# Weighted one-hots for four tokens at a time in a scatter by matmul

## The chip, the cores and the metric
The kernel runs on one core of one Trainium2 chip, as one program. The metric is the device time of one execution in microseconds. TensorE (PE) does the matmuls, VectorE (DVE) and ScalarE (ACT) the elementwise work, GpSimd (POOL) some gathers, SyncE (SP) starts most transfers. Each engine works through its own queue in order, and semaphores hold an instruction until what it reads has been written and what it overwrites has been read.

## The reference
One decoder layer on a sequence of 1024 tokens of width 1024: a gMLP and an S5 state space branch with an output projection, then a retrieval layer with 8 heads over 16384 experts (128 x 128 product keys), then a final norm. The retrieval layer is what matters here:

```
s = einsum('thcd,hckd->thck', q, keys); top_s, top_i = top_k(s, 16)
cand_s = top_s[:, :, 0, :, None] + top_s[:, :, 1, None, :]      # 16 x 16 sums of a head
best_s, pos = top_k(cand_s, 16); idx = the experts of these;  g = softmax(best_s)
act = gelu(einsum('thkd,td->thk', u_tab[idx], t));  y = einsum('thk,thkd->td', g * act, v_tab[idx])
```

Each token so has 128 (8 x 16) pairs of an expert index and a weight g. All arithmetic is in float32.

## The kernel before
Tokens are worked on in 8 blocks of 128. The last three go the way of the reference: the rows of their experts are gathered by GpSimd, multiplied and summed (`side_work`). For the first five (640 tokens) the kernel computes all 16384 experts densely on TensorE, and needs their weights as a matrix G of tokens by experts that is zero where an expert wasn't chosen.

The first third of the span is the two branches, then come output projections (`outproj`), scores (`score`) and routes (`route`, with `topk`: runs of MAX8, FIND_INDEX8 and MATCH_REPLACE8 on VectorE). A route gives for each token 128 first key numbers (`I32t`), 128 second ones (`J16`) and 128 weights (`gT`), transposed so that a column is a token and its 128 choices lie across the partitions. `scatter` (L678 and on) makes G from them. It takes eight tokens at a time:

- `hot` (L685): one VectorE operation compares the number of a column with `J16`; fp16, [128, 128 keys, 8 tokens], the tokens innermost. So one token's one-hot lies in every eighth element, 16 bytes apart.
- `a1` (L690): VectorE, for four tokens at a time, the one-hot of the first key; fp32, token by token in a row. Two buffers.
- `b1` (L694 or L698): the one-hot of the second key times the weight. For a pair of tokens either VectorE makes it in one operation of 256 elements, or ScalarE in two activations of 128. Which one is set by a number for each block, `dv`: every dv-th pair is VectorE's. Six buffers of two tokens.
- L700: for each token one product of `b1` and `a1` on TensorE, 128 x 128, which the trace shows as two matmul instructions; L703: ScalarE copies the results of eight tokens to `GS` in two operations; L706: SyncE stores 32 tokens' worth in `G_d`.

After the scatter come the pairs of dense stages: `stage1` (L959, products with the first table and gelu), `weigh` (L978, times G) and `stage2` (L997, L1006, products with the second table), over 128 groups of experts, with `side_work` between them. `stage1` of the first five groups may run ahead of the last scatter.

The order in which pieces of the blocks' work are issued (routes r0 to r7, scatters s0 to s4, scores, projections) comes from the table `plan` in CFG: a start and a length for each item, into which its steps are spread. A scheduler that simulates the engines then orders the instructions of each queue. The routes of gather blocks 5 and 6 are issued among the last scatters; they read their scores back from memory (`scr`) in buffers that share the tag `hs` with `hot`.

Of the kernel before, what the change touches and what calls it, by code (L numbers as in the profile page):

```python
# [8 lines left out]
F32 = mybir.dt.float32  # L9
# [6 lines left out]
AF = mybir.ActivationFunctionType  # L16
ALU = mybir.AluOpType
# [4 lines left out]
P = 128  # L22
# [16 lines left out]
QG = 4  # L39
GP = 2  # L40
FMAX = 3.0e38
CFG = dict(xo=[2, 3, 4, 0, 1], gt=3, ss=7, hs=2, b1=6, nw=6, raw=1, ngb=3, rows=4, lead=5, per=6.3, dv=[6, 9, 9, 2, 99], early=2,
           hp=600, eo=(2, 4), em={2: 'pppxx', 4: 'Xpp'}, seg=4, plan=dict(
    op0=(-238.2, 44.5), sb0=(-21, 248.8), m5=(-490.1, 3.4), r0=(234.1, 82.1), op1=(132.1, 27.3), op2=(292.7, 7.7),
    sb1=(310, 10.8), op3=(364.9, 36.8), r1=(301.9, 79), s0=(261.5, 137.5), sb2=(303.2, 61.7), zv=(372.6, 16.7),
# [3 lines left out]
    gt=(858.2, 122), rel=(739, 334), s4=(981.8, 131.5), r5=(916.4, 58.6), r6=(989.9, 124.6), ld=(776, 675.7),  # L49
# [11 lines left out]
def bcast(ap, axis, n):  # L61
    shape = list(ap.shape)
    shape.insert(axis, n)
    idx = [slice(None)] * len(ap.shape)
    idx.insert(axis, None)
    return ap[tuple(idx)].to_broadcast(shape)
# [30 lines left out]
@with_exitstack  # L97
def tile_hybrid_layer(ctx: ExitStack, tc: tile.TileContext, a, out, cfg=CFG):
    nc = tc.nc
    V, A, G, T = nc.vector, nc.scalar, nc.gpsimd, nc.tensor  # L100
# [25 lines left out]
    def bankB(name):  # L126
        return psB.tile([P, 2, 512], F32, tag="b", name=name)
# [43 lines left out]
    def slotS(shape, name, dt=F32):  # L171
        return sS.tile(shape, dt, tag="k8", name=name)
# [36 lines left out]
    early = {}  # L209
# [351 lines left out]
    ss = []  # L561
# [116 lines left out]
    def scatter(b, I32t, J16, gT):  # L678
        t0 = b * P
        for q in range(4):  # L680
            GS = [slotS([P, NE // 2, 32], f"GS{b}_{q}_{i}") for i in range(2)]
            for t8 in range(4):
                s1 = q * 32 + t8 * 8
                hot = kp.tile([P, P, 8], F16, tag="hs", name=f"hot{b}_{s1}", bufs=cfg["hs"])
                V.tensor_tensor(hot, iot8, bcast(J16[:, s1:s1 + 8], 1, P), op=ALU.is_equal)  # L685
                pg = bankB(f"pgs{b}_{s1}")
                for o in range(8):
                    if o % 4 == 0:
                        a1 = kp.tile([P, 4, P], F32, tag="a1", name=f"a1_{b}_{s1 + o}", bufs=2)
                        V.tensor_tensor(a1, bcast(iot, 1, 4), bcast(I32t[:, s1 + o:s1 + o + 4], 2, P), op=ALU.is_equal)  # L690
                    if o % 2 == 0:
                        b1 = kp.tile([P, 2, P], F32, tag="b1", name=f"b1_{b}_{s1 + o}", bufs=cfg["b1"])
                        if (s1 + o) // 2 % cfg["dv"][b] == 0:
                            V.tensor_tensor(b1, hot[:, :, o:o + 2].rearrange("p j t -> p t j"),  # L694
                                            bcast(gT[:, s1 + o:s1 + o + 2], 2, P), op=ALU.mult)
                        else:
                            for n in range(2):
                                A.activation(b1[:, n], hot[:, :, o + n], AF.Copy,  # L698
                                             scale=gT[:, s1 + o + n:s1 + o + n + 1])
                    T.matmul(pg[:, o // 4, (o % 4) * P:(o % 4 + 1) * P], b1[:, o % 2], a1[:, o % 4], start=True, stop=True)  # L700
                pgv = pg.rearrange("p a (t i) -> p i (a t)", t=4)
                for i in range(2):
                    A.copy(GS[i][:, :, t8 * 8:t8 * 8 + 8], pgv[:, i * 64:(i + 1) * 64])  # L703
                yield
            for i in range(2):
                nc.sync.dma_start(G_d[i * 16:(i + 1) * 16, :, b * 4 + q, :].rearrange("g p c -> p g c"),  # L706
                                  GS[i].rearrange("p (g e) t -> p g (e t)", e=QG))
# [93 lines left out]
    def put(b):  # L801
        yield from scatter(b, *ijg.pop(b))
# [243 lines left out]
    def lead(i0, i1):  # L1046
        for i in range(i0, i1):
            yield from stage1(i)
# [23 lines left out]
    def prep_steps(n):  # L1072
# [17 lines left out]
        gt=(gt2_row, 1, "m5"), rel=(release, NDB, "gt op7 sb7"), ld=(lambda: lead(0, L), 2 * L, "rel"))  # L1090
# [13 lines left out]
    while left:  # L1104
# [3 lines left out]
        _, n, need = items[item]  # L1108
# [384 lines left out]
```

## Time and profile before

| | us |
|---|---|
| median of 3 runs | 2657.55 (2655.81 to 2659.86) |
| the profiled execution | 2655.86 |
| its span, first to last instruction | 2653.9 |
| TensorE busy | 2538.1 (96%) |
| VectorE busy | 2267.8 (85%) |
| ScalarE busy | 1312.8 (49%) |
| GpSimd busy | 1180.9 (44%) |

Shares of busy time are means over stages that differ: the stretches are in the first group of the rows below. Scatter instructions run from 354 to 860 us. A duration in a row is that of one instruction; on a full engine the next one starts before the last has quite ended, so the distance from start to start is shorter. A wait names who was late, by the profile's inference from semaphores.

### The profile page before, as it was taken

Reading aid. Unit: us, or ns where it says so; the run is one execution under the profiler, and the core shown is the slowest. Engines: PE = TensorE matmul, PEld = TensorE weight load, DVE = VectorE, ACT = ScalarE, POOL = GpSimd, SP = SyncE. Lnnn points to the kernel's source line nnn. Section 1 sums busy time; section 2 is a strip of 40 time slices with the busy share of each in tenths; the row PEclk is TensorE's granted clock in tenths of the full one; section 3 lists DMA queues with packets and bytes.
Section 4 is the critical chain, followed back from the end, with each engine's and each line's share of the span. In section 5 each row is a group of like instructions: output and inputs, shape, how many; then the busy total and the mean of one; then the engine's idle time right before and its main releaser. Section 6 shows DMA issues by size and latency. Waiting matters only on the chain. (4 is left out here: it accounts for less than half of the span.)

```text
span 2653.9 us, 39049 instructions
## 1 busy us (share of the span) xinstructions
PE 2538.1 (96%) x14119; PEld 2168.1 (82%) x14119; DVE 2267.8 (85%) x4215; ACT 1312.8 (49%) x2315; POOL 1180.9 (44%) x842
## 2 busy tenths in 40 slices
PE   6999999999877999999999999999999999999997
PEld 2548677678666898989999989999999988999986
DVE  7984699869899888789989888889999888899898
ACT  2311246568868377773222577762223767732222
POOL 0001000000000177676667578766665767776660
PEclk9996999999988999999999999999999999999999
DMA  9546233444636699999999999899998999999993
GB/s 362 108 121 217 101 122 104 126 136 135 181 118 193 218 328 326 343 327 364 341 340 375 325 336 330 331 354 364 341 355 326 334 345 343 325 368 345 343 365 139
DMA packets 301761, 726.85 MB, mean 274 GB/s; under 512 B 42448, under 2 KB 133072, under 8 KB 301152
## 3 DMA queue, kind: packets, MB, share of 16 engines
q0 software_dynamic: 112832, 411.09, 42.4%
q1 hardware_dynamic: 165600, 254.48, 28.6%
q10 hardware_dynamic: 23136, 58.79, 6.2%
q8 instruction: 111, 1.82, 0.3%
q14 instruction: 82, 0.67, 0.1%
HBM read 660.70 MB, written 62.39 MB: 272 GB/s over the span
## 5 line engine op out<-in xcount | busy, mean ns | idle before, releaser
L888 POOL DMA_INDIRECT ru<-in_peer_u_dram,ix x384 | 637.7, 1661 | 897.6 <-issue 745.1
L959 PE MATMUL pa<-Th,u 128*128 128x320 f32 x4096 | 911.3, 310 | 4.9 <-DVE u L936 3.1
L959 PEld LDWEIGHTS pa<-Th,u 128*128 128x128 f32 x4096 | 688.4, 188 | 8.7 <-DVE u L936 3.6
L888 POOL DMA_INDIRECT rv<-in_peer_v_dram,ix x384 | 522.8, 1361 | 257.4 <-DVE gacc L916 168.0
L959 PE MATMUL pa<-Tl,u 128*128 128x320 f32 x2048 | 633.4, 309 | 0.0
L899 DVE TENSOR_TENSOR ru<-ru,hn 128x2048 f32<-128x2048 f32 x192 | 438.6, 2289 | 113.1 <-DMA ru<-in_peer_u_dram,ix 106.6
L894 ACT ACTIVATE jk<-ru 128x1024 bf16<-128x1024 f32 x384 | 405.4, 1056 | 213.2 <-issue 167.7
L916 DVE SCALAR_TENSOR_TENSOR gacc<-rv,act,gacc 128x1024 f32<-128x1024 f32 x381 | 489.2, 1284 | 6.4 <-DVE u L936 0.4
L1006 PE MATMUL pd<-v,wh 128*128 128x512 f32 x1280 | 402.6, 390 | 3.2 <-ACT wh L980 1.6
L997 PE MATMUL res<-v,wh 128*128 128x512 f32 x1280 | 400.7, 390 | 0.8 <-ACT wh L980 0.8
L959 PEld LDWEIGHTS pa<-Tl,u 128*128 128x128 f32 x2048 | 385.3, 188 | 1.7
L1006 PEld LDWEIGHTS pd<-v,wh 128*128 128x128 f32 x1280 | 238.8, 188 | 52.5 <-ACT wh L980 2.5
L997 PEld LDWEIGHTS res<-v,wh 128*128 128x128 f32 x1280 | 239.6, 188 | 50.4 <-ACT wh L980 1.6
L961 ACT ACTIVATE w<-pa 128x320 f32<-128x320 f32 x256 | 108.7, 431 | 333.7 <-PE pa L959 311.9
L698 ACT ACTIVATE b<-hot,gT 128x128 f32<-128x128 f16 x520 | 233.5, 537 | 61.0 <-PE pgs L700 36.0
L1006 PE MATMUL pd<-v,wl 128*128 128x512 f32 x640 | 248.7, 390 | 1.7 <-DVE wl L982 1.6
L997 PE MATMUL res<-v,wl 128*128 128x512 f32 x640 | 248.1, 389 | 1.3 <-DVE wl L982 1.3
L935 ACT CAST u<-ur 128x1024 fp32r<-128x1024 f32 x128 | 133.5, 1043 | 205.3 <-DMA ur<-in_peer_ut_dram 79.0
L700 PE MATMUL pgs<-a,b 128*128 128x128 f32 x1280 | 188.9, 299 | 46.2 <-DVE a L690 19.3
L700 PEld LDWEIGHTS pgs<-a,b 128*128 128x128 f32 x1280 | 169.9, 207 | 68.4 <-ACT b L698 35.3
L936 DVE TENSOR_TENSOR u<-ur,u 128x1024 fp32r<-128x1024 f32 x128 | 156.3, 1221 | 29.7 <-ACT u L935 23.2
L943 ACT CAST v<-vr 128x1024 fp32r<-128x1024 f32 x128 | 133.7, 1045 | 94.1 <-DMA vr<-in_peer_v_dram 76.8
(349 smaller groups left out, 3050.4 us busy)
## 6 DMA issues: line engine op xcount, KB each, us to landing
vr<-in_peer_v_dram SPq DMA_DIRECT2D x128, 512.0 KB
ur<-in_peer_ut_dram SPq DMA_DIRECT2D x128, 512.0 KB
G_d<-GS SPq DMA_DIRECT2D x40, 1024.0 KB
Gt<-G_d ACTq DMA_DIRECT2D x64, 640.0 KB
wada<-in_w_ada_dram SPq DMA_DIRECT2D x17, 1024.0 KB
wo<-in_w_out_dram SPq DMA_DIRECT2D x8, 1024.0 KB
ru<-in_peer_u_dram,ix POOLq DMA_INDIRECT x384
rv<-in_peer_v_dram,ix POOLq DMA_INDIRECT x384
```

The source lines that it names most:

```text
L698: A.activation(b1[:, n], hot[:, :, o + n], AF.Copy, scale=gT[:, s1 + o + n:s1 + o + n + 1])
L700: T.matmul(pg[:, o // 4, (o % 4) * P:(o % 4 + 1) * P], b1[:, o % 2], a1[:, o % 4], start=True, stop=True)
L888: G.indirect_dma_start(out=row[:, e], out_offset=None, in_=a[src], in_offset=bass.IndirectOffsetOnAxis(ap=ix[:, s0 + e:s0 + e + 1], axis=0))
L894: A.activation(junk, row[:, e], AF.Copy, accum_out=act[:, s + e:s + e + 1])
L899: V.tensor_mul(row, row, bcast(hn, 1, GP))
L916: V.scalar_tensor_tensor(ac, row[:, e], w, ac, op0=ALU.mult, op1=ALU.add)
L935: A.copy(u[:, 0], ur)
L936: V.tensor_tensor(u[:, 1], ur, u[:, 0].bitcast(F32), op=ALU.subtract)
L943: A.copy(v[:, 0], vr)
L959: T.matmul(pa[:, :NN], l[:, k, :], r[:, k, ns], start=(k == 0 and m == 0), stop=(k == KD - 1 and m == 2))
L997: T.matmul(res[tb][n], l[:, ts], r[:, n * 512:(n + 1) * 512], start=(g == 0 and q == 0 and m == 0), stop=(g == NGR - 1 and q == QG - 1 and ...
L1006: T.matmul(po, l[:, ts], r[:, n * 512:(n + 1) * 512], start=(q == 0 and m == 0), stop=(q == QG - 1 and m == 2))
```

## The change
`b1` of two tokens becomes `b4` of four, with three buffers in place of six. Where VectorE makes it, one operation of 512 elements covers four tokens: the loop over keys is the outer one and that over tokens the inner one, so it reads four fp16 values in a row of `hot` and the four weights, and writes each value to another token's row, 512 bytes on. ScalarE's activations are as before, one for each token. The numbers `dv` now count quads, and are 3, 4, 4, 1, 3 where they were 6, 9, 9, 2, 99 for pairs. The plan is the same.

```diff
-CFG = dict(xo=[2, 3, 4, 0, 1], gt=3, ss=7, hs=2, b1=6, nw=6, raw=1, ngb=3, rows=4, lead=5, per=6.3, dv=[6, 9, 9, 2, 99], early=2,
+CFG = dict(xo=[2, 3, 4, 0, 1], gt=3, ss=7, hs=2, b4=3, nw=6, raw=1, ngb=3, rows=4, lead=5, per=6.3, dv=[3, 4, 4, 1, 3], early=2,
...
-                    if o % 2 == 0:
-                        b1 = kp.tile([P, 2, P], F32, tag="b1", name=f"b1_{b}_{s1 + o}", bufs=cfg["b1"])
-                        if (s1 + o) // 2 % cfg["dv"][b] == 0:
-                            V.tensor_tensor(b1, hot[:, :, o:o + 2].rearrange("p j t -> p t j"),
-                                            bcast(gT[:, s1 + o:s1 + o + 2], 2, P), op=ALU.mult)
-                        else:
-                            for n in range(2):
-                                A.activation(b1[:, n], hot[:, :, o + n], AF.Copy,
-                                             scale=gT[:, s1 + o + n:s1 + o + n + 1])
-                    T.matmul(pg[:, o // 4, (o % 4) * P:(o % 4 + 1) * P], b1[:, o % 2], a1[:, o % 4], start=True, stop=True)
+                    if o % 4 == 0:
+                        b4 = kp.tile([P, 4 * P], F32, tag="b4", name=f"b4_{b}_{s1 + o}", bufs=cfg["b4"])
+                        wide = (s1 + o) // 4 % cfg["dv"][b] == 0
+                        bt = b4.rearrange("p (t j) -> p t j", t=4)
+                        if wide:
+                            V.tensor_tensor(b4.rearrange("p (t j) -> p j t", t=4), hot[:, :, o:o + 4],
+                                            bcast(gT[:, s1 + o:s1 + o + 4], 1, P), op=ALU.mult)
+                    if not wide:
+                        A.activation(bt[:, o % 4], hot[:, :, o], AF.Copy, scale=gT[:, s1 + o:s1 + o + 1])
+                    T.matmul(pg[:, o // 4, (o % 4) * P:(o % 4 + 1) * P], bt[:, o % 4], a1[:, o % 4], start=True, stop=True)
```

## Rows read from the trace of the kernel before

**Rows 1.** Stretches: length, busy PE PEld DVE ACT POOL (instructions), clock, DMA share, GB/s

```profile
350.00:640.00 290.00, 282.02 (x1741) 215.86 (x1739) 256.23 (x1139) 192.09 (x422) 0.00 (x0) 0.99 0.41 128
640.00:720.00 80.00, 65.04 (x468) 56.04 (x467) 72.68 (x135) 79.09 (x183) 0.00 (x0) 1.00 0.58 167
720.00:860.00 140.00, 103.33 (x624) 90.18 (x623) 125.57 (x574) 102.59 (x221) 0.00 (x0) 0.85 0.55 161
900.00:2600.00 1700.00, 1692.08 (x9502) 1543.31 (x9501) 1475.22 (x1205) 840.84 (x1328) 1163.35 (x773) 1.00 0.93 341
```

**Rows 2.** Waits, 350 to 640 us: who for whom, us in total, times, longest

```profile
ACT b L698 <- PE pgs L700: 31.3, 19, 7.9
...
DVE a L690 <- PE pgs L700: 12.8, 10, 7.3
```

**Rows 3.** Waits, 640 to 720 us, of PE and of DVE

```profile
PE pgs L700 <- ACT b L698: 5.5, 7, 0.9
PE pgs L700 <- DVE a L690: 4.6, 6, 1.4
...
DVE hot L685 <- ACT b L698: 3.7, 9, 1.1
DVE b L694 <- PE pgs L700: 1.3, 2, 1.2
```

**Rows 4.** Waits, 720 to 860 us, of PE, ACT and DVE

```profile
PE pgs L700 <- DVE a L690: 11.5, 10, 2.4
PE pgs L700 <- ACT b L698: 9.5, 7, 4.2
...
ACT b L698 <- DVE hot L685: 14.2, 8, 3.7
...
DVE m L1378 <- DMA scr<-sc_d: 11.9, 6, 4.9
```

**Rows 5.** Groups by line, DVE, 350 to 860 us: busy us, mean ns, idle before

```profile
L690 DVE TENSOR_TENSOR a<-iot,It 128x512 f32<-128x512 f32 x160 | 108.7, 684 | 14.1 <-PE pgs L700 13.9
L685 DVE TENSOR_TENSOR hot<-iot,Jt 128x1024 f16<-128x1024 f16 x80 | 54.8, 686 | 11.6 <-ACT b L698 11.5
L694 DVE TENSOR_TENSOR b<-hot,gT 128x256 f32<-128x256 f16 x60 | 36.2, 609 | 1.5 <-PE pgs L700 1.3
```

**Rows 6.** Stretches, instructions that touch `b` alone: PE, PEld, DVE, ACT

```profile
350.00:640.00 290.00, 74.94 (x568) 70.44 (x568) 12.86 (x21) 113.37 (x251) 0.99 0.41 128
640.00:720.00 80.00, 56.04 (x395) 48.09 (x393) 21.57 (x36) 55.61 (x124) 1.00 0.58 167
720.00:860.00 140.00, 57.95 (x320) 51.40 (x320) 1.78 (x3) 64.50 (x148) 0.85 0.55 161
```

**Rows 7.** Timeline, ACT, from 820 us: start, us, instruction, count

```profile
820.13 5.93 ACT L698 ACTIVATE b<-hot,gT 128x128 f32<-128x128 f16 x14
825.96 1.03 ACT L836 CAST Th<-t 128x1024 fp32r<-128x1024 f32 x1
```

**Rows 8.** Timeline, DVE, from 682 us

```profile
682.41 1.14 DVE L694 TENSOR_TENSOR b<-hot,gT 128x256 f32<-128x256 f16 x2
683.46 0.69 DVE L690 TENSOR_TENSOR a<-iot,It 128x512 f32<-128x512 f32 x1
684.06 0.69 DVE L685 TENSOR_TENSOR hot<-iot,Jt 128x1024 f16<-128x1024 f16 x1
```

**Rows 9.** Groups by line and form, DVE, up to 360 us

```profile
L450 DVE TENSOR_TENSOR X<-X,t_s 128x128 f32<-128x128 f32 x30 | 11.9, 395 | 0.0
...
L621 DVE TENSOR_TENSOR ss<-ysT,sg 128x512 f32<-128x512 f32 x4 | 4.4, 1092 | 4.3 <-ACT sg L620 4.3
```

**Rows 10.** Timeline, DVE, from 522 us

```profile
522.57 1.10 DVE L621 TENSOR_TENSOR ss<-ysT,sg 128x512 f32<-128x512 f32 x1
523.47 0.11 DVE L1380 MATCH_VALUE_LOAD ca<-bs,ca 128x8 f32 x1
```

## The prediction

> **What bounds the kernel now.** I read the table by stages first. From 900 us on TensorE is busy in 1692.1 of 1700 us at granted clock 1.00, so that part is a fixed block of matmuls: whatever moves its start moves the end by as much [rows 1]. The scatter, the only code that changes, lies before it, and its three stretches are not alike. From 350 to 640 us TensorE is 97% busy with projections and scores as well (282.0 of 290 us), and there ScalarE's one-hots wait for TensorE 31.3 us and VectorE's `a1` 12.8 us: the makers of one-hots are ahead of their reader [rows 1, 2]. From 640 to 720 us ScalarE is full (79.1 of 80 us), VectorE has 7.3 us left (72.7 of 80), TensorE is at 65.0. [...] The waits say the same: from 640 to 720 us TensorE waits 5.5 us for `b` of ScalarE and 4.6 us for `a1` of VectorE, from 720 to 860 us 9.5 and 11.5 us [rows 3, 4]. So two engines share the bound in some 220 us, and the change takes work from one and gives it to the other.
>
> **How many one-hots change hands.** Each token has one weighted one-hot (`b`), so there are 640. The rule is a modulus per block. Before, of 64 pairs in a block, every 6th, 9th, 9th, 2nd and only the first: 11 + 8 + 8 + 32 + 1 = 60 pairs, 120 tokens on VectorE, 520 on ScalarE; the counts of operations agree [rows 5, 6]. After, of 32 quads, every 3rd, 4th, 4th, every one, every 3rd: 11 + 8 + 8 + 32 + 11 = 70 quads, 280 tokens on VectorE and 360 on ScalarE. Block 3 is made by VectorE alone, and block 4, nearly all ScalarE's before, by a third.
>
> **ScalarE: what goes.** 160 activations. A run of 14 takes 5.83 us from its first start to the next instruction, 0.416 us each [rows 7]: 160 x 0.416 = 67 us less.
>
> **VectorE: what one quad costs.** What counts on a full engine is start to start. A contiguous 512-element tensor_tensor (`a1`) starts the next after 0.60 us; two pairs of 256 elements take 1.05 us together, 0.525 each, which is nearly as much as twice the elements of `a1` [rows 8]. The pair reads fp16 every 16 bytes and writes in a row; `a1` does neither and also has a broadcast operand, so it is the spaced read that costs. The quad reads runs of four, so that cost should go. But it writes fp32 values 512 bytes apart, one to each token in turn. The trace has a spaced write of the same size: L621 reads two contiguous operands of 512 and writes every 32 bytes, and takes 1092 ns against 684 for `a1` [rows 5, 9]; its next instruction starts after 0.90 us [rows 10]. L450, 128 elements written (and read) every 128 bytes, takes 395 ns, more than half of `a1` with a quarter of its elements, so a wider spacing doesn't make it free [rows 9]. I take 0.91 us, by L621, the nearest row. The bounds: 0.60 if the write is free (`a1`), 1.05 if a quad costs two pairs.
> [...]
>
> **The sum, by stretches.** VectorE in all: 70 x 0.91 = 63.7 less 60 x 0.525 = 31.5, that is +32 us (+10.5 at 0.60, +42 at 1.05).
> - 350 to 640 us: 568 matmul instructions at two for each token are 284 tokens [rows 6], and the quads that the other two stretches leave over are 21 in place of 21 pairs: 21 x (0.91 - 0.525) = +8 us on VectorE. TensorE is the bound and the makers are ahead of it, so this hides under it; if it did not, it would cost up to 8. I take +1.
> - 640 to 720 us: 124 one-hots by ScalarE and 36 pairs, 196 tokens [rows 6]. With block 3 at one half and the other block at one ninth, n/2 + (196 - n)/9 = 72 gives n = 129: all of block 3 and 67 of block 1. After: 128 + 17 = 145 tokens on VectorE, 36 quads instead of 36 pairs, 36 x (0.91 - 0.525) = +13.9 us. VectorE then has 72.7 + 13.9 = 86.6 us in a stretch of 80. ScalarE falls by (124 - 51) x 0.416 = 30 us to 49 and bounds nothing. So the bound passes from ScalarE to VectorE: +7 us. What VectorE itself waits here (3.7 us for ScalarE to leave a `hot` buffer, 1.3 us before a pair) [rows 3] is small and partly stays, since a quad waits for the last of four matmuls of its buffer.
> - 720 to 860 us: 148 one-hots and 3 pairs. After, 11 quads of block 4 and some two of block 1: 13 x 0.91 - 3 x 0.525 = +10 us on VectorE, 136 of 140. The cover is thin: VectorE's 11.9 us of waiting for scores of the gather blocks (`scr`) [rows 4], and the routes of blocks 5 and 6, whose steps may slip past 860 us. Against that ScalarE loses 46 activations, 19 us, and TensorE's wait of 9.5 us for `b` should go; but ScalarE waited 14.2 us for `hot` of VectorE [rows 4], so what it gains it can only use when VectorE is in time. Between -10 and +10 us; I take 0.
> The buffers stay at 12 tokens (three of four for six of two). A buffer comes free only after four matmuls; with ScalarE ahead this costs it waiting, which is not the bound. A quad that waits holds up `hot`, `a1` and route steps behind it in VectorE's queue, and through them TensorE; `a1` with two buffers waits first (12.8 us early on [rows 2]), so I put nothing on it.
> Sum: +1 + 7 + 0 = +8 us on the profiled execution's 2655.9 us (span 2653.9 and 2.0 around it): 2663.9. The median of the runs is 1.7 us above that execution: 2665.5.
>
> **The rivals.**
> - The spaced write is free, a quad costs 0.60 us: chance 0.24. From 640 to 720 us VectorE gains 36 x 0.075 = 2.7 us, 75.4 in all, and with ScalarE out of the way the stretch takes about 76: -4. From 720 to 860 us +6.2 us on VectorE against 9.5 us of TensorE's waits for `b`: -3 at least, and -8 if the scores' waits cover the 6.2. Together about -10 of the median: 2647.5. [...] Against it: L621 and L450.
> - The quad costs 0.91 but ScalarE was the one that mattered: chance 0.14. TensorE's 5.5 and 9.5 us of waits for `b` and VectorE's 3.7 for `hot` go, and the +24 us on VectorE from 640 to 860 us push routes of blocks 5 and 6 past the scatter, where VectorE has 225 us to spare (1475 busy of 1700 [rows 1]): -8, 2649.5. Against it: VectorE's order mixes routes and scatter, and TensorE waits more for `a1` than for `b` late on.
> - Nothing that can be measured: chance 0.22, within 5 us of 2657.5. The two effects cancel, +7 against the waits for `b`.
> - Slower, beyond the forecast: VectorE becomes the bound all through, because a spaced write at 512 bytes costs a quad 1.05 us or more. From 640 to 720 us 36 x 0.525 = +19 us, of which 12 come to light, from 720 to 860 us +12 us, of which the 11.9 us of `scr` waits hide little, and 3 of the early 10: about +24, 2681.5. It decides from some 0.8 us a quad, where VectorE's 72.7 + 36 x (q - 0.525) passes the 80 us that ScalarE takes now (q = 0.73) by more than ScalarE's waits give back. Chance 0.12; the forecast itself 0.28.
>
> **How the numbers follow.** A difference under 0.2% (5.3 us) is about what a measurement of this kernel can tell from none. Forecast 0.28 and the dear quad 0.12 are slower: 0.40. The free write and ScalarE's relief are faster: 0.38. The rest, 0.22, is the same. Time 2665.5. Its own range is 2659 to 2676; the range of 8 in 10 takes in both the faster cases and most of the dear quad: 2641 to 2682.
>
> **What would show it.** The quad's row beside L621's 1092 ns: near 690 the step is wrong and the first rival holds. VectorE at 95% or more from 640 to 860 us with `pgs` waiting for VectorE and hardly for `b`: the forecast's bound. ScalarE's `b` at 360 operations, some 150 us in all. The first dense matmuls near 850 us or later by what the end moves; if the end moves and they don't, the cause lies outside the scatter and the whole sum is wrong.

## The result, and the profile after

| | before | after |
|---|---|---|
| median, us (runs) | 2657.55 (11) | 2674.91 (11) |
| lowest and highest | 2635.03, 2661.94 | 2648.62, 2677.88 |
| ratio, 95% interval | | 1.0062 [1.0039, 1.0086] |
| span of the profiled execution | 2653.9 | 2672.2 |

The change makes the kernel slower by 0.62%, 16.5 us of 2657.55 (10 to 23 by the interval). The forecast was +8. The ratios here and below leave out two executions at a low mean granted clock, one of the kernel before (3171.47 us, clock 0.748) and the traced one of the experiment e12 (3677.10 us, 0.643). The stretches after, with the columns of [rows 1]:

```profile
350.00:640.00 290.00, 274.31 (x1642) 205.92 (x1641) 255.42 (x1102) 169.61 (x359) 0.00 (x0) 0.97 0.39 122
640.00:720.00 80.00, 62.33 (x494) 56.55 (x493) 77.36 (x144) 51.48 (x109) 0.00 (x0) 1.00 0.53 152
720.00:860.00 140.00, 102.22 (x604) 87.50 (x603) 132.83 (x541) 85.31 (x183) 0.00 (x0) 0.82 0.58 170
```

From 640 to 860 us VectorE is 97% and 95% busy, where it had 91% and 90%; ScalarE falls from 79.1 to 51.5 us in the first of the two. In the stretch that I had called TensorE's, TensorE's own busy time falls from 282.0 to 274.3 of 290 us. The groups by line, 350 to 880 us, the columns of [rows 5]:

```profile
L699 ACT ACTIVATE b<-hot,gT 128x128 f32<-128x128 f16 x360 | 160.2, 527 | 73.9 <-PE pgs L700 36.1 <-DVE hot L685 32.2 <-issue 4.2
...
L696 DVE TENSOR_TENSOR b<-hot,gT 128x512 f32<-128x512 f16 x70 | 74.5, 1065 | 0.0
L685 DVE TENSOR_TENSOR hot<-iot,Jt 128x1024 f16<-128x1024 f16 x80 | 55.4, 696 | 3.5 <-ACT b L699 3.5
```

70 quads of 1065 ns, near L621's 1092 [rows 9] and far from `a1`'s 684 [rows 5]. In VectorE's timeline the next operation starts 0.88 us after the quad:

```profile
683.38 1.05 DVE L696 TENSOR_TENSOR b<-hot,gT 128x512 f32<-128x512 f16 x1
684.26 0.69 DVE L685 TENSOR_TENSOR hot<-iot,Jt 128x1024 f16<-128x1024 f16 x1
```

Now the waits after, in the three stretches of [rows 2 to 4]. From 350 to 640 us:

```profile
ACT b L699 <- PE pgs L700: 28.1, 13, 8.3
...
DVE a L690 <- PE pgs L700: 11.2, 10, 2.8
...
PE pgs L700 <- DVE a L690: 9.9, 7, 3.6
```

From 640 to 720 us there is no wait of PE for ScalarE's `b` any more (5.5 us in [rows 3]), and the one for `a1` has gone from 4.6 to 15.2:

```profile
PE pgs L700 <- DVE a L690: 15.2, 24, 1.2
```

From 720 to 860 us:

```profile
ACT b L699 <- DVE hot L685: 21.1, 7, 6.3
...
PE pgs L700 <- DVE a L690: 18.7, 16, 4.1
...
PE pgs L700 <- ACT b L699: 5.8, 3, 4.3
...
DVE m L1378 <- DMA scr<-sc_d: 5.6, 4, 3.7
```

**Where the time went.** Fixed stretches of the clock don't hold the same work in both kernels. Stretches between four events come nearer to that: the first and the last transpose of a route's weights (L791, blocks 0 and 4), the last copy of a route's key table (L795, block 4, held until an earlier block's table has been read), and the last copy of scatter results (L703). In these rows the two times after the durations are the first and the last start. Before:

```profile
L791 PE MATMUL pij<-ident,g x5: 273/273/273, 351.1 to 656.1; 128*128 128x128 f32 x5
...
L795 ACT COPY It<-pij x5: 266/267/394, 351.5 to 718.1; 128x128 f32<-128x128 f32 x5
...
L703 ACT COPY GS<-pgs x160: 558/588/729, 366.8 to 857.9; 128x512 f32<-128x512 f32 x160
```

After:

```profile
L791 PE MATMUL pij<-ident,g x5: 272/272/273, 354.3 to 667.4; 128*128 128x128 f32 x5
...
L795 ACT COPY It<-pij x5: 244/267/268, 354.6 to 736.3; 128x128 f32<-128x128 f32 x5
...
L703 ACT COPY GS<-pgs x160: 558/587/659, 367.5 to 875.9; 128x512 f32<-128x512 f32 x160
```

| | before | after | moved | forecast |
|---|---|---|---|---|
| start to first route | 351.1 | 354.3 | +3.2 | 0 |
| first to last route | 305.0 | 313.1 | +8.1 | +1 |
| last route to last table | 62.0 | 68.9 | +6.9 | +7 |
| last table to last result | 139.8 | 139.6 | -0.2 | 0 |
| last result to the end | 1796.0 | 1796.3 | +0.3 | 0 |

The first line lies before any changed instruction; over the traces below it runs from 349.9 to 354.8, which is an execution's own spread, and in two of them (e7, e10) it is 331, which the last section takes up. For one order of the queues the next three distances can be trusted to about 1 us: e10 and e11 have the same scatter as before, and measure 304.0 and 304.1, 62.0 and 61.9, 140.7 and 140.4. Another order moves the events among the work. The scatter's matmuls in the three stretches are 624, 337 and 320 before and 608, 344 and 328 after; e1, which has before's shares in quads, has 608 and 353 in the first two, which take 299.1 and 71.2 us. So the sum of the first two stretches (367.0 before, 382.0 after) is surer than its split. By these events the changed part of the program has lost 14.8 us, in two places. These are the stretches between the events (columns of [rows 1]), before:

```profile
351.10:656.10 305.00, 296.12 (x1862) 229.20 (x1862) 269.95 (x1163) 207.38 (x454) 0.00 (x0) 0.99 0.42 128
656.10:718.10 62.00, 48.80 (x341) 41.65 (x340) 56.60 (x95) 61.89 (x144) 0.00 (x0) 1.00 0.58 167
718.10:857.90 139.80, 103.13 (x614) 89.00 (x613) 124.82 (x575) 103.52 (x225) 0.00 (x0) 0.85 0.56 165
```

And after:

```profile
354.30:667.40 313.10, 296.55 (x1845) 228.18 (x1845) 277.43 (x1160) 191.99 (x408) 0.00 (x0) 0.97 0.40 123
667.40:736.30 68.90, 48.50 (x349) 41.79 (x349) 67.53 (x96) 37.41 (x78) 0.00 (x0) 1.00 0.57 161
736.30:875.90 139.60, 105.28 (x627) 91.98 (x626) 132.49 (x581) 85.47 (x181) 0.00 (x0) 0.82 0.56 165
```

First stretch: VectorE has 7.5 us more to do and idles as long as before (305.0 - 269.95 = 35.1; 313.1 - 277.43 = 35.7), so the stretch grew by about as much. TensorE is busy as long (296.1, 296.6) and its idle time grows from 8.9 to 16.6. Most of that growth lies in one spot. TensorE's timeline there, in brackets its idle time ahead of the row and what ended it, before and after:

```profile
492.62 4.60 PE L700 MATMUL pgs<-a,b 128*128 128x128 f32 x24 [1.40 <-ACT sc L748]
```

```profile
501.10 3.78 PE L700 MATMUL pgs<-a,b 128*128 128x128 f32 x16 [3.99 <-DVE b L696]
508.50 2.04 PE L700 MATMUL pgs<-a,b 128*128 128x128 f32 x8 [3.62 <-DVE a L690]
```

After, VectorE itself waits 4.9 us for TensorE up to 493 us (for `mx`). Then it works without a pause, with steps of a route ahead of the quad and of the next `a1` in its queue, TensorE stands still twice, and the granted clock falls to 0.50, the lower of its two levels (in steps of 0.25 us the traces of before and after stand at 1.00 or 0.50; other values, in 24 and 30 of some 10,600 steps, only where it changes):

```profile
500.00:510.00 10.00, 5.28 (x23) 5.02 (x24) 10.00 (x51) 3.80 (x9) 0.00 (x0) 0.50 0.62 170
```

Second: ScalarE filled 61.9 of 62.0 us, now VectorE fills 67.5 of 68.9 and ScalarE 37.4; here the bound did pass over. Third: VectorE's 7.7 us more go into its idle time (15.0, now 7.1), half of that its waits for `scr` (11.9, now 5.6).

### The profile page after: what moved, and what is told of

Read it like the earlier page. It is cut to its first block, busy times and chain, and to the rows that moved or that the text cites. A ratio compares the mean times of both kernels' runs of the same rounds, so it can differ in the third digit from the quotient of the medians.

```text
span 2672.2 us, 38860 instructions
## 1 busy us (share of the span) xinstructions
PE 2544.5 (95%) x14119; PEld 2174.3 (81%) x14119; DVE 2297.9 (86%) x4225; ACT 1255.8 (47%) x2159; POOL 1165.4 (44%) x842
## 4 chain that ended last, share of the span: by engine, by line
PE 75%; DVE 18%; DMA 2%; ACT 2%; issue 2%; POOL 0%; ACTq 0%; DVEq 0%; POOLq 0%
PE pa L959 31%; PE res L997 16%; PE pd L1006 16%; PE po L637 3%; DVE a L690 2%; PE pq L736 2%; PE pzs L361 2%; PE pgs L700 2%; DVE b L696 1%; DVE hot L685 1%; DVE ixs L1379 1%; PE py L578 1%; PE pg L617 1%; DVE ixs L1382 1%; DMA scr<-sc_d 1%
## 5 line engine op out<-in xcount | busy, mean ns | idle before, releaser
L888 POOL DMA_INDIRECT ru<-in_peer_u_dram,ix x384 | 623.1, 1623 | 922.2 <-PE res L997 678.7
L699 ACT ACTIVATE b<-hot,gT 128x128 f32<-128x128 f16 x360 | 160.2, 527 | 73.9 <-PE pgs L700 36.1
```

The costliest lines, as they stand in the source:

```text
L699: A.activation(bt[:, o % 4], hot[:, :, o], AF.Copy, scale=gT[:, s1 + o:s1 + o + 1])
L888: G.indirect_dma_start(out=row[:, e], out_offset=None, in_=a[src], in_offset=bass.IndirectOffsetOnAxis(ap=ix[:, s0 + e:s0 + e + 1], axis=0))
```

## Experiments

Each was timed beside the kernel before, on the same chip. Its median was 2658.53 with e0, e1, e2 and e6, 2655.14 with e3, e4, e5 and e7, 2657.30 with e9 to e12. Ratios are to it. My theory was the forecast's: the quad has L621's price, and VectorE bounds block 3. The main rival was that the early shares, whose cost I had put under TensorE, are what costs.

| | VectorE's part | median | ratio, 95% interval |
|---|---|---|---|
| after | 70 quads, `dv` 3, 4, 4, 1, 3 | 2674.91 | 1.0062 [1.0039, 1.0086] |
| e1 | 31 quads, 6, 9, 9, 2, 99 | 2659.81 | 1.0002 [0.9979, 1.0025] |
| e2 | 44 quads, 3, 4, 4, 2, 99 | 2668.07 | 1.0039 [1.0019, 1.0058] |
| e3 | 47 quads, 6, 9, 9, 1, 99 | 2652.28 | 0.9999 [0.9979, 1.0018] |
| e4 | 41 quads, 6, 9, 9, 2, 3 | 2660.77 | 1.0021 [0.9999, 1.0044] |
| e12 | 36 quads, 99, 99, 99, 1, 99 | 2665.91 | 1.0029 [1.0012, 1.0046] |
| e9 | 36 pairs, 99, 99, 99, 2, 99 | 2666.75 | 1.0035 [1.0017, 1.0054] |
| e5 | 140 pairs, 3, 4, 4, 1, 3 | 2678.28 | 1.0096 [1.0072, 1.0120] |
| e6 | after's quads, written in a row | 2693.18 | 1.0136 [1.0094, 1.0177] |
| e7 | 15 groups of eight without `hot` | 2660.63 | 1.0022 [1.0004, 1.0041] |
| e10 | before, 27 operations without use | 2653.55 | 0.9995 [0.9976, 1.0015] |
| e11 | before, 33 operations without use | 2655.47 | 0.9995 [0.9972, 1.0019] |

**e0: the price of a spaced operand by itself.** The changed kernel with eight VectorE operations of each of twelve kinds behind its last work; one run gave 2745.04 us, of which only the rows matter.

```diff
...
+    for _ in range(8):
+        V.tensor_tensor(c[:, :512].rearrange("p (t j) -> p j t", t=4), hot[:, :, 0:4], bcast(sc[:, 0:4], 1, P), op=ALU.mult)
+    for _ in range(8):
+        V.tensor_tensor(c[:, :512].rearrange("p (j t) -> p j t", t=4), hot[:, :, 0:4], bcast(sc[:, 0:4], 1, P), op=ALU.mult)
...
+        V.tensor_tensor(c[:, :1024].rearrange("p (j t) -> p j t", t=2)[:, :, 0], d[:, :512], f[:, :512], op=ALU.mult)
...
+        V.tensor_tensor(c[:, :1024].rearrange("p (j t) -> p j t", t=4)[:, :, 0:2], d[:, :512].rearrange("p (j t) -> p j t", t=2), f[:, :512].rearrange("p (j t) -> p j t", t=2), op=ALU.mult)
...
+        V.tensor_tensor(c[:, :1024].rearrange("p (j t) -> p j t", t=4)[:, :, 0], d[:, :256], f[:, :256], op=ALU.mult)
...
```

> The changed kernel with 96 more VectorE operations on scratch data behind the dense stages, eight of each of twelve kinds, whose results go nowhere; only their durations count. Theory (each value written to another 16-byte line costs, whatever the distance): a contiguous 512-element tensor_tensor 0.60 us from start to start, the pair 0.525, the quad 0.90, the quad with its write in a row 0.60, 512 values written every 8 bytes near 0.60, pairs of values every 16 bytes near 0.60, 256 values written every 16 bytes as dear per value as the quad. Rival (the quad's read, runs of four with gaps, is what costs): the quad with its write in a row stays near 0.90 and the spread write of contiguous operands falls to 0.60. A tensor_scalar of 128 with two scalars per partition: 0.15 to 0.25 us.

Its groups by line (mean ns behind the comma). L1158 is contiguous; L1162 the quad; L1164 the quad written in a row; L1168 writes one value every 8 bytes, L1170 two every 16 bytes, L1172 (256 elements) one every 16 bytes:

```profile
L1162 DVE TENSOR_TENSOR bench<-bench,bench 128x512 f32<-128x512 f16 x8 | 8.2, 1031 | 0.2
...
L1168 DVE TENSOR_TENSOR bench<-bench,bench 128x512 f32<-128x512 f32 x8 | 5.5, 693 | 0.3
L1170 DVE TENSOR_TENSOR bench<-bench,bench 128x512 f32<-128x512 f32 x8 | 5.5, 693 | 0.3
L1164 DVE TENSOR_TENSOR bench<-bench,bench 128x512 f32<-128x512 f16 x8 | 5.5, 692 | 0.3
L1158 DVE TENSOR_TENSOR bench<-bench,bench 128x512 f32<-128x512 f32 x8 | 5.5, 682 | 0.0
L1172 DVE TENSOR_TENSOR bench<-bench,bench 128x256 f32<-128x256 f32 x8 | 4.9, 610 | 0.3
```

The read in runs of four costs next to nothing (692, contiguous 682), the write is the whole price (1031): the change took the penalty off the read and put it on the write. 512 bytes apart costs an element as much as 16 does, some 0.7 ns (1031 against 682 for 512 elements, 610 against e10's 424 for 256), and two values in 16 bytes are already free (693). So at these spacings the theory holds, and its rival falls (692).

**e1: the form alone.** Quads with before's shares.

```diff
-CFG = dict(xo=[2, 3, 4, 0, 1], gt=3, ss=7, hs=2, b4=3, nw=6, raw=1, ngb=3, rows=4, lead=5, per=6.3, dv=[3, 4, 4, 1, 3], early=2,
+CFG = dict(xo=[2, 3, 4, 0, 1], gt=3, ss=7, hs=2, b4=3, nw=6, raw=1, ngb=3, rows=4, lead=5, per=6.3, dv=[6, 9, 9, 2, 99], early=2,
```

The edits of `dv` below are shown by that entry of the line alone.

> The changed kernel with VectorE's shares of before: every 6th, 9th, 9th, 2nd quad and the first, 6 + 4 + 4 + 16 + 1 = 31 quads, 124 tokens. Theory (the added time is VectorE's larger share): VectorE's part of the one-hots is 31 x 0.895 = 28 us against 31.5 before, so the time is that of before within 5 us, 2653 to 2660. Rival (buffers of four tokens make ScalarE wait, or the new order of instructions costs): still slower, 2665 to 2675.

1.0002: the quad as such and the coarser buffers cost and gain nothing that can be measured (-6 to +7 us by the interval). The cost of the change is its shares.

**e2: the early shares alone** (blocks 0 to 2; blocks 3 and 4 as before).

```diff
-dv=[3, 4, 4, 1, 3]
+dv=[3, 4, 4, 2, 99]
```

> The changed kernel with the new shares in blocks 0, 1 and 2 alone (every 3rd, 4th, 4th quad), block 3 every 2nd and block 4 the first: 44 quads. Theory (the early stretch cost 11 us of the 18, since VectorE's routes set its pace and not TensorE): 2664 to 2670. Rival (blocks 3 and 4 cost it): 2654 to 2660.

1.0039, more than half of the whole. Its stretches between the same events:

```profile
351.50:664.70 313.20, 296.64 (x1846) 228.29 (x1846) 277.40 (x1160) 191.91 (x408) 0.00 (x0) 0.97 0.40 123
664.70:726.00 61.30, 49.61 (x354) 43.01 (x353) 56.03 (x82) 61.00 (x140) 0.00 (x0) 1.00 0.62 175
726.00:866.40 140.40, 109.11 (x609) 94.80 (x609) 124.98 (x575) 102.19 (x223) 0.00 (x0) 0.79 0.57 166
```

Against before +8.2, -0.7 and +0.6: after's first loss, with the same two waits of 3.99 and 3.62 us, and no other. Against e1, which has the quads and before's shares, the first two stretches together are 4.2 us longer (374.5, 370.3) and the ratio is 0.0037 higher, about 10 us. The term that I had hidden under TensorE stands here by itself. ScalarE fills the second stretch as it did before (61.0 of 61.3).

**e3 and e4: block 3 alone, block 4 alone.**

```diff
-dv=[3, 4, 4, 1, 3]
+dv=[6, 9, 9, 1, 99]
```

```diff
-dv=[3, 4, 4, 1, 3]
+dv=[6, 9, 9, 2, 3]
```

> The changed kernel's quads with the new share in block 3 alone (every quad), the others as in the shares of before: 47 quads. Theory (block 3 passes from ScalarE's bound to VectorE's, 7 us): 2662 to 2668. Rival (only the early blocks cost): 2655 to 2661.

> The changed kernel's quads with the new share in block 4 alone (every 3rd), the others as in the shares of before: 41 quads. Theory (there ScalarE's relief pays for VectorE's load): 2655 to 2661. Rival (VectorE is the bound there too, 10 us of load): 2664 to 2670.

In e3's trace the stretch of block 3 is as forecast VectorE's, which is full for most of it, with ScalarE idle:

```profile
649.20:723.30 74.10, 52.44 (x368) 44.94 (x367) 68.86 (x98) 43.87 (x93) 0.00 (x0) 0.98 0.56 162
```

But its time is that of before (0.9999), below the 2662 to 2668 that was expected. Its first two stretches together are 373.3 us, 3.0 more than in e1; the interval of its ratio can't tell that from nothing. From first route to last result it took 512.9 us against 506.8, and the dense part, whose instructions are the same, 1785.4 against 1796.0; over the variants that part runs from 1785.4 to 1802.8, over three executions with before's scatter from 1796.0 to 1800.8. e1, too, has its own early stretch (299.1 us, then 71.2). So an order of the queues may have its own few us elsewhere, and block 3's +7, plain between the traces of e2 and after (61.3, 68.9), isn't confirmed as a term by itself in time. e4: 1.0021 with an interval that touches 1, its last stretch 140.0 us: as forecast, nothing resolved. Over e1 the three parts add to 0.0053 of ratio (0.0037, -0.0003, 0.0019), and all together cost 0.0060; each of these differences is uncertain by some 0.003.

**e5: after's shares by pairs**, in before's code.

```diff
-dv=[6, 9, 9, 2, 99]
+dv=[3, 4, 4, 1, 3]
```

> The kernel before, with pairs, and the new numbers 3, 4, 4, 1, 3 for pairs: 140 pairs, 280 tokens by VectorE as in the changed kernel. Theory (time follows VectorE's load): 140 x 0.525 = 73.5 us against 63 for 70 quads at 0.90, so 5 to 10 us slower than the changed kernel, 2679 to 2686. Rival (the share costs whatever the price of an operation, and quads bring nothing): 2672 to 2678.

1.0096: with the same tokens the pair is dearer than the quad. 140 x 0.525 = 73.5 us of VectorE against 70 x 0.91 = 63.7, 9.8 us; the ratios differ by 0.0034, 9.0 us. Their intervals overlap, and 2678.3 lies between the two expected ranges; the traces agree with the theory (531.7 us from first route to last result, after 521.6).

**e6: the quad written in a row.** TensorE then reads the weights of a token 16 bytes apart, and the price lies with it (a median weight load of 307 ns, in after 192).

```diff
-                        bt = b4.rearrange("p (t j) -> p t j", t=4)
+                        bt = b4.rearrange("p (j t) -> p t j", t=4) if wide else b4.rearrange("p (t j) -> p t j", t=4)
...
-                            V.tensor_tensor(b4.rearrange("p (t j) -> p j t", t=4), hot[:, :, o:o + 4],
+                            V.tensor_tensor(b4.rearrange("p (j t) -> p j t", t=4), hot[:, :, o:o + 4],
```

> The changed kernel, same shares; VectorE's quads are written in a row, four tokens side by side, and the matmul reads every fourth value of them instead, 16 bytes apart. Theory (the spaced write makes the quad dear, and its price makes the change slow): the quad falls from 1059 to about 690 ns, VectorE has 70 x 0.30 = 21 us less to do, and the time falls by 15 to 25 us from the changed kernel's, to 2650 to 2660. Rival (TensorE pays for the spaced read of its weights): its weight loads for these 560 instructions get longer than 192 ns and give the gain back, 2670 or more.

The instructions that touch `b` (min/median/max in ns), in after:

```profile
L700 PEld LDWEIGHTS pgs<-a,b x1280: 186/192/338, 365.2 to 875.0; 128*128 128x128 f32 x183
L700 PE MATMUL pgs<-a,b x1280: 272/275/582, 365.2 to 875.1; 128*128 128x128 f32 x183
L696 DVE TENSOR_TENSOR b<-hot,gT x70: 1040/1059/1127, 359.7 to 862.9; 128x512 f32<-128x512 f16 x70
```

And in e6:

```profile
L700 PEld LDWEIGHTS pgs<-a,b x1280: 186/307/338, 365.7 to 892.0; 128*128 128x128 f32 x183
L700 PE MATMUL pgs<-a,b x1280: 272/382/602, 365.7 to 892.1; 128*128 128x128 f32 x183
L696 DVE TENSOR_TENSOR b<-hot,gT x70: 668/685/698, 360.2 to 878.9; 128x512 f32<-128x512 f16 x70
```

The quad falls from 1059 to 685 ns and the median weight load, over all tokens, rises from 192 to 307: slower than after by 0.74% of ratio. The free quad, my first rival, can't be had this way. One more thing shows here: VectorE's busy time from first to last route is 271.4 us, 1.4 above before's, and yet TensorE still waits up to 3.6 us for a quad and up to 3.5 us for an `a1`, in after 3.99 and 3.62 near 500 us:

```profile
PE pgs L700 <- DVE a L690: 16.5, 17, 3.5
...
PE pgs L700 <- DVE b L696: 6.2, 3, 3.6
```

So waits of this length (here from 350 to 900 us) don't come from the price of a quad alone. That what VectorE's queue holds ahead of it counts as well is my reading.

**e7: no `hot` in part of the groups.** In 15 groups of eight VectorE compares and weights a token in one tensor_scalar, from a second fp32 copy of the key table; before's code, ScalarE makes the rest.

```diff
...
+                            if direct:
+                                V.tensor_scalar(b1[:, n], iot, J32[:, c:c + 1], gT[:, c:c + 1], op0=ALU.is_equal, op1=ALU.mult)
+                            else:
+                                A.activation(b1[:, n], hot[:, :, o + n], AF.Copy, scale=gT[:, c:c + 1])
...
```

> The kernel before, with VectorE's share (120 tokens) in whole groups of eight: 15 groups, 3 + 2 + 2 + 8 + 0. In such a group there is no hot; each token is one tensor_scalar of 128 elements, column number equal to the token's second key, times its weight, both scalars per partition. ScalarE copies the second keys once more for each block, in fp32. Theory (time follows VectorE's load in the scatter): at 0.20 us from start to start 120 x 0.20 - 15 x 0.60 = 15 us in place of 31.5, so 8 to 17 us faster than before, 2641 to 2650. Rival (a tensor_scalar with two scalars takes 0.35 us from start to start, as in the row of operations that write the same tile): 33 us, no change, 2654 to 2661.

Its timeline shows four of them in 1.11 us and its groups 120 of 340 ns; VectorE saved some 9 us from first route to last result (442.0 busy, before 451.4), and the kernel got slower, 1.0022 (8 to 17 us faster was expected).

```profile
PE pgs L701 <- DVE a L692: 28.6, 25, 2.3
...
DVE hot L687 <- ACT b L700: 14.1, 16, 1.9
```

These waits (330 to 860 us) suggest why: whole groups by one engine and then by the other make the two wait in turn. Before, over the scatter, the first was 19.3 us and the second 11.5 [rows 5]. No run shows it by itself.

**e9: VectorE relieved early.** Before's code with the early shares nearly at nothing, 12.8 us off VectorE from first to last route (7.9 below e1, whose stretch holds as many scatter matmuls).

```diff
-dv=[6, 9, 9, 2, 99]
+dv=[99, 99, 99, 2, 99]
```

> The kernel before, with pairs, and VectorE nearly out of blocks 0, 1 and 2 (the first pair only): 36 pairs in place of 60, 12.6 us less on VectorE and 20 us more on ScalarE, all early. Theory (VectorE's load sets the pace of the early stretch): 7 to 13 us faster than before, 2643 to 2650. Rival (the two engines are balanced there, and ScalarE's 20 us take back what VectorE gives): within 5 us of before.

It should have been faster if VectorE alone set the early pace, and within 5 us if the two engines are balanced; it is slower, 1.0035, 9 us. Its stretches:

```profile
354.50:658.60 304.10, 292.96 (x1830) 224.12 (x1829) 257.19 (x1138) 217.91 (x486) 0.00 (x0) 0.99 0.40 125
658.60:729.70 71.10, 58.82 (x373) 49.23 (x372) 58.94 (x98) 68.36 (x156) 0.00 (x0) 0.95 0.56 162
```

VectorE's idle time takes up the relief (46.9 us, before 35.1); its wait for ScalarE to leave `hot`, 350 to 640 us, goes from 6.8 to 13.4:

```profile
DVE hot L685 <- ACT b L698: 13.4, 8, 4.3
```

Its second stretch is that of e1 (71.2 us, 155 operations of ScalarE), so its length there needn't be owed to the shares. The first tells more. With 608 scatter matmuls in it, as here, it takes 299.1 to 299.2 us in e1, e3 and e4 (before's shares), 304.1 in e9 (by pairs; less on VectorE, more on ScalarE) and 313.2 in e2 (the reverse; 16 other matmuls more). So the early shares of before lie near a balance: a move either way made the stretch longer. That more load on one engine alone would do so isn't shown. Of the 9 us the trace shows 4.6 from first route to last result; the rest lies ahead of it (3.4) and behind it (1.5), where nothing was changed.

**e12: the same early shares, block 3 whole, by quads.**

```diff
-dv=[3, 4, 4, 1, 3]
+dv=[99, 99, 99, 1, 99]
```

> The changed kernel's quads in block 3 alone (every quad), one quad in each of the others: 36 quads. VectorE has 36 x 0.90 = 32 us, as much as before, but 11 us less early and 13 more in block 3; ScalarE 12 us less in all, 20 more early and 27 less in block 3. Theory (early load costs 1:1, block 3's passes from one engine to the other): 3 to 10 us faster than before, 2647 to 2654. Rival (early load is hidden, block 3's is not): 2660 to 2668.

1.0029, beside e9's 1.0035: relief early is no gain, and block 3 whole or half again makes no difference that can be measured. The time lies in the rival's range, but its reason, a cost of block 3 by itself, isn't what e3 shows.

**e10 and e11: load on VectorE alone.** Operations of 256 elements that nobody waits for, ahead of each of VectorE's pairs in the first three blocks (e10, below) or in the last two (e11, `b >= 3`), to part VectorE's load from ScalarE's relief.

```diff
+                            if b < 3:
+                                dm = kp.tile([P, 2, P], F32, tag="dm", name=f"dm{b}_{s1 + o}")
+                                V.tensor_tensor(dm, bcast(iot, 1, 2), bcast(iot, 1, 2), op=ALU.mult)
```

> The kernel before, with one more VectorE operation behind each pair of blocks 0, 1 and 2 whose result nobody reads (256 elements in a row): 27 x 0.33 = 9 us more on VectorE, nothing else changed. Theory (VectorE's load early goes through to the end): 7 to 11 us slower than before. Rival (TensorE's fixed work hides it, as the prediction had it; what cost the early stretch was the coarser buffer or the new split): within 4 us of before.

> The same operation behind each pair of blocks 3 and 4: 33 x 0.33 = 11 us more on VectorE late, of which 10.7 in block 3. Theory (there ScalarE is full and VectorE has 7 us left from 640 to 720 us): 3 to 7 us slower. Rival (VectorE is the pace there as early): 9 to 13 us slower.

Both missed their purpose. Since their input is ready from the start, they were ordered ahead of the scatter; in e10 (in e11 from 252.6 to 278.6 us):

```profile
L698 DVE TENSOR_TENSOR dm<-iot x27: 411/424/426, 234.3 to 249.7; 128x256 f32<-128x256 f32 x27
```

They suggest that VectorE has room there (0.9995 both), and give the repeats of the scatter used above; nothing on the question.

No variant beats before by more than its interval.

## Why the prediction was right in part

Slower was right, and so was the price that it rests on; the amount came out at twice the forecast, mostly by one term.

- **The quad's price: right.** 0.91 us forecast, 0.88 measured from start to start. With it the free write (0.60 us; its chance of 0.24 was an estimate that no row of before supports) and the dear quad (1.05) fall. The reason given for the pair's price holds too, though `a1` also writes in a row, other than the prediction says: 256 elements without a spaced operand take 424 ns (e10's row), the pair 609 [rows 5].
- **The counts: right.** 24, 34 and 12 quads between the events, where I had 21, 36 and 13; ScalarE's `b` at 360 operations, 160 us where I wrote some 150.
- **350 to 640 us, "this hides under it ... I take +1": wrong, the step that failed.** +8.1 in after and +8.2 in e2, where no other share is new, and 10.4 us by its ratio (5 to 15). The size of the load was right (+8; 7.5 measured); the cover was not there. I read the 31.3 and 12.8 us of waiting for TensorE [rows 2] as a reserve. After, VectorE still waits 11.2 us for TensorE, and in the same stretch TensorE waits 9.9 us for `a1` and 4.0 for a quad (the row of 3.99). Both kinds of wait stand side by side at different moments, and room at one moment doesn't serve at another: 35 us of VectorE's idle time stayed idle. That TensorE was 97% busy only said that it rarely waited yet; its 8.9 us of idle time became 16.6, of which 7.6 are the two waits near 500 us. That the time lost (8.1) is so near the load added (7.5) doesn't show that load comes out one for one: e6 has waits nearly as long (3.6 and 3.5 us, from 350 to 900 us) with 1.4 us of added load. I named the cost of this failing (up to 8) and didn't use it.
- **640 to 720 us, +7 by a passing bound: right in the trace** (+6.9; VectorE 67.5 of 68.9 us full, ScalarE 37.4). By itself (e3) it is not confirmed in time, and that 6.9 meets 7 so well is in part luck, since this stretch is 9.2 us longer in e1 with before's shares.
- **720 to 860 us, 0: right** (-0.2), and the cover was the one named: `scr` waits from 11.9 to 5.6. The relief of ScalarE showed (TensorE's wait for `b` 9.5 to 5.8) and bought nothing, since the wait for `a1` rose from 11.5 to 18.7: the second rival falls.
- **"The start moves the end by as much": right for after** (last result +18.0, span +18.3), but not to be leaned on for a variant: e3's dense part is 10.6 us shorter than before's.

The parts of the forecast add to +8 and those measured to +14.8; the spans differ by 3.2 us more ahead of the scatter and 0.3 behind it. By these parts the forecast would have been 2672.6 with the early term at 8.1.

Left open: whether load on VectorE alone, without ScalarE's relief, costs the same early on (e10 was to tell); how much of the early loss is the load and how much the order of VectorE's queue near 500 us, since no run changed the order by itself; and block 3's share in time. That e1 gains 5.9 us early and gives back 9.2 behind it is in part a matter of where the last route falls: 33 of TensorE's matmuls pass from the first stretch to the second (1829 and 374; before 1862 and 341).

## What to carry to other kernels

TensorE's busy share of 97% was here no cover for 7.5 us more work on VectorE, which feeds it (the stretch grew by 8.1): ask whether the feeding engine's idle time is usable at the moment of the new work, and where both engines wait for each other in one stretch, don't put the load at nothing. When a layout is turned to make a read cheap, price the write at the same time; here two 4-byte values in 16 bytes were free to write (693 ns) and one was not (1031). Where two engines share a job that each fills in turn, test the share in both directions before moving it: here less and more on VectorE were both slower by 0.4%.

## What the hardware showed unexpectedly

In the traces read here, but for those of e7 and e10, some 44 us of the first third, with TensorE busy throughout, run at the lower of its two clock levels (before, 0.50 from 199.5 to 243.5 us and 1.00 from 243.75). Before, the stretches from 190 us on (columns of [rows 1]); TensorE had waited 2.5 us for VectorE's `X` at 196 us:

```profile
190.00:200.00 10.00, 7.51 (x32) 4.63 (x31) 9.97 (x15) 0.60 (x1) 0.00 (x0) 0.97 0.11 26
...
210.00:230.00 20.00, 20.00 (x86) 18.43 (x85) 11.19 (x21) 2.23 (x4) 0.00 (x0) 0.50 0.37 85
230.00:250.00 20.00, 20.00 (x105) 18.15 (x104) 5.63 (x11) 2.04 (x4) 1.61 (x16) 0.66 0.58 149
```

In e7's traced execution, whose code is the same up to there and where TensorE had idled nearly as long (2.3 us):

```profile
190.00:200.00 10.00, 7.66 (x33) 4.52 (x32) 9.97 (x15) 0.60 (x1) 0.00 (x0) 1.00 0.09 14
...
210.00:230.00 20.00, 20.00 (x153) 17.85 (x152) 17.01 (x33) 2.78 (x5) 1.88 (x18) 1.00 0.91 221
```

At granted clock 1.00 the same 20 us hold nearly twice the matmuls (153, 86). Such an execution is some 20 us shorter (e7's first route at 330.9 us, before's at 351.1), which is about the gap between a kernel's lowest runs and its median (before, 2635.03 and 2657.55). What decides between the two wasn't found; it is why the profiles are compared here by distances between events and not by spans.
